# Residual of the second half in a place of its own, and copies for two sets of weight sums, both issued ahead of the first half's MLP products

## The chip, the cores and the metric

The kernel runs on one core of one Trainium2 chip. The core has a matrix engine (TensorE, PE, with its weight loads as PEld), a vector engine (DVE), a scalar engine (ACT), GpSimd (POOL) and SyncE (SP), which here does nothing but issue DMAs. Sixteen DMA engines move the data. DMAs are issued from two places: SP (the queue called SPq, hardware_dynamic) and POOL (POOLq, software_dynamic). Each engine works through its own instructions in order and waits on semaphores for the others. The metric is the device time of one launch in microseconds (us); lower is better.

## What is computed

A trunk of two layers on 1024 tokens of width 1024, in float32. Layer 0 mixes tokens with a gated linear recurrence, layer 1 with a causal Conformer convolution; each mixer is followed by a squared-ReLU MLP of inner width 4096, with a residual and a layer norm after each.

```python
for i in range(DEPTH):
    if i % N_MIXERS == 0:
        mix = hgrn2_mixer(x, ...)
    else:
        mix = conformer_conv_mixer(x, ...)
    x = layer_norm(DEEPNORM_ALPHA * x + mix, ln_mix_g[i], ln_mix_b[i])
    ff = jnp.square(jax.nn.relu(x @ ffn_w1[i])) @ ffn_w2[i]
    x = layer_norm(DEEPNORM_ALPHA * x + ff, ln_ffn_g[i], ln_ffn_b[i])

def conformer_conv_mixer(h, w_pw1, b_pw1, w_dw, b_dw, ln_g, ln_b, w_pw2, b_pw2):
    a, gate = jnp.split(h @ w_pw1 + b_pw1, 2, axis=-1)
    u = a * jax.nn.sigmoid(gate)
    u = depthwise_causal_conv(u, w_dw) + b_dw          # 31 taps
    u = jax.nn.silu(layer_norm(u, ln_g, ln_b))
    return u @ w_pw2 + b_pw2
```

The change lies in layer 1. The residual that it speaks of is `DEEPNORM_ALPHA * x` in front of the first of the two norms.

## The kernel before

**Numbers.** Every float32 factor of a product is split into a high part and a remainder, and each product is three matmuls: high by high, high by low, low by high (`product`, line 329). One such matmul, with a tile of 128x128 and 512 columns, is what the profile calls `ps<-xa,wa` and the like. 24 of them, eight tiles of the inner dimension by three, make one 128x512 result.

**Fewer products.** The large products are cut into 2x2 blocks and done with seven block products in place of eight; the seven "forms" are numbered in `ORDER` (line 45). Forms 6, 5, 7 and 3 of a weight are sums of its four blocks. For the second MLP weight w2 these sums are made in DRAM, one set for each of the eight column groups of each layer: `block_sums` (line 393) copies blocks into a DRAM tile of four places (`sum_w` in the profile) with two plain DMAs of 1 MB, and adds to it with three accumulating DMAs, which POOL issues. The list `to_sum` (line 408) has sixteen sets. Fourteen are made in layer 0, the last two, groups 6 and 7 of layer 1, later. Where the argument `after` is given, a marker comes first: a DMA of two elements from `after` into the tile, which holds the copies back until `after` has been written. They then go through SP's queue.

**Layer 1** works on two halves of 512 tokens, `half` 0 and 1. The string `SEQ` (line 40) gives the order of its steps, and the loop at line 1680 runs them:

- P0j and P1j: the pointwise input product of channel block j. It leaves behind the convolution of that block as background work: 19 taps on DVE, 12 taps that ACT multiplies and POOL adds. The result is turned by PE into `ct[half]`, the tile `y` of 16 KB a partition.
- N, F, S: `normalise` (line 1554), the layer norm of the convolution; `finish` (line 1579), which turns it back and applies SiLU into `sT[half]`; `second` (line 1600), the output product with w_pw2, the residual and the norm. The weights of all these steps come through `wa` (a `Slots` object, line 60; six places of 8 KB).
- UA0 to UA4: the first half's MLP up-products `up_half(1, i, 0, ...)` for column groups 0 to 4, four blocks of w1 each. They fill PE while the second half's convolution runs in the background. Thirteen of the w1 blocks lie already split in DRAM (`ready`): two DMAs of 512 KB each, with no work on ACT or DVE. Block k of UA is loaded as `wa` has a free place, six blocks behind the one that used it.
- E, UB and L: the first two forms of the remaining groups for the first half, the second half's up-products for groups 0 to 4, and groups 5 to 7 for both halves. The down-products with w2 follow.

**Places.** SBUF is laid out by hand in KB of a partition (`view`, line 274). `ct[0]` lies at 32 to 48, `ct[1]` at 48 to 64. After its last turn in `finish`, `ct[half]` is loaded anew with the residual from `kept[half]` in DRAM, four DMAs of 512 KB on SP (line 1596); `second` scales it by ALPHA and adds the bias on DVE (line 1605), adds each product and normalises in place. Later tiles take the same places over: `xf6` at 32, `s7` at 48, `first` at 56, and the slots of the last MLP.

**Order.** After line 1019 the order of the instructions on each engine is not the program's: a scheduler places them by its own simulated time. Only the order on each engine is fixed so; what an engine waits for is decided by semaphores. Consecutive DMAs of SP take eight semaphores in turn, so that a DMA also waits for the landing of the eighth before it. In layer 1 the order of the steps on PE is P00 to P17 (with N0, F0, S0 in between), then UA0 to UA4, N1, F1 and S1 (with E5 to E7 in between), then UB0.

Of the kernel before, what the change touches and what calls it, by code (L numbers as in the profile page):

```python
# [8 lines left out]
F32 = mybir.dt.float32  # L9
# [3 lines left out]
ALU = mybir.AluOpType  # L13
# [249 lines left out]
def body(ctx, tc, d, out):  # L263
# [126 lines left out]

    sums = {}

    def block_sums(name, layer, c, after=None, gap=0):

        t = sums[name, layer, c] = dram.tile([4, P, 1024], F32, name=f"sum_{name}{layer}{c}")
        v, w = t.rearrange("a p n -> p a n"), d[name][layer, c].rearrange("a p n -> p a n")
        queue = nc.sync if after is not None else nc.gpsimd
        if after is not None:
            nc.sync.dma_start(out=t[0:4:2, 0, 0:1], in_=after)
        queue.dma_start(out=v[:, 0:2], in_=w[:, 0:4:2])  # L400
        later(gap // 2, lambda: queue.dma_start(out=v[:, 2:4], in_=w[:, 0:2]))
        parts = [lambda: nc.gpsimd.dma_start(out=v[:, 0:2], in_=w[:, 2:4], accum_op=ALU.add)]
        for i in (2, 3):
            parts.append(lambda i=i: nc.gpsimd.dma_start(out=v[:, i], in_=v[:, i - 1], accum_op=ALU.add, max_dma_last_dim=4096))
        for i, part in enumerate(parts):
            later((i + 1) * gap, part)
# [817 lines left out]
    class LateUp(Up):  # L1224


        def __init__(self, xs):
            self.layer, self.xf = 1, xs
            self.zs, self.ws = bank((1, 5, 2, 6)), bank((3, 7, 0, 4))
            self.c = ring((132, 134, 136, 138, 128, 130), wide_t, "c")  # L1230
            self.hr = ring((16, 24, 0, 8), (2, 2, HT), "hr")
            self.t = ring(run(112, 4, 2), (2, 256), "ht")
            self.p = ring((56,), (2, HT), "first")
            self.of = {}

        def bring(self, c):
# [317 lines left out]
    def normalise(half):  # L1554

        for job in conv[KB * half : KB * half + KB]:
            bg.flush(job)
        while late:
            late.pop(0)()
        mv = stat.tile([P, NTB, 5], F32, tag="mv4", name="mv", bufs=2)  # L1560
        for t in range(NTB):
            vector.bn_aggr(mv[:, t, 0:2], cs[half][:, t])
        vector.tensor_scalar(out=mv[:, :, 2:3], in0=mv[:, :, 1:2], scalar1=LN_EPS, scalar2=None, op0=ALU.add)
        nc.gpsimd.tensor_tensor(out=mv[:, :, 3:4], in0=mv[:, :, 2:3], in1=nhalf[:, :NTB].rearrange("p (a b) -> p a b", b=1), op=ALU.pow)
        vector.scalar_tensor_tensor(out=mv[:, :, 4:5], in0=mv[:, :, 0:1], scalar=-1.0, in1=mv[:, :, 3:4], op0=ALU.mult, op1=ALU.mult)
        normed[0] = 1
        if half == 1:
            for of in to_sum:
                block_sums(*of, mv[:2, 0, 4:5])
        gate[1] = [mv[:, 0, 4:5]] * 2  # L1570
        for n in range(2):
            for t in range(NTB):
                cv = ct[half][:, t, n * HT : (n + 1) * HT]
                if n == 0 and t % 2:
                    vector.tensor_scalar(out=cv, in0=cv, scalar1=mv[:, t, 3:4], scalar2=mv[:, t, 4:5], op0=ALU.mult, op1=ALU.add)
                else:
                    nc.scalar.activation(cv, cv, AF.Identity, bias=mv[:, t, 4:5], scale=mv[:, t, 3:4])

    def finish(half):

        st = sT[half]

        def one(j):
            pt = rings["aux"]()
            for t in range(NTB):
                tensor.transpose(pt[:, t * P : (t + 1) * P], ct[half][:, t, j * P : (j + 1) * P], ident)
            z = big("z")
            sg = big("r")
            gj, bj = par[:, CLG + j : CLG + j + 1], par[:, CLB + j : CLB + j + 1]
            nc.scalar.activation(sg, pt, AF.Sigmoid, bias=bj, scale=gj)  # L1590
            nc.scalar.activation(z, pt, AF.Identity, bias=bj, scale=gj)
            vector.tensor_tensor(out=z, in0=z, in1=sg, op=ALU.mult)
            split(st[:, 0, j, :], st[:, 1, j, :], z)
            if j == KB - 1:
                for t in range(NTB):
                    nc.sync.dma_start(out=ct[half][:, t, :], in_=kept[half][t])

        bg.chores += [lambda j=j: (one(j), one(j + 1)) for j in range(0, KB, 2)]

    def second(half):  # L1600

        y = ct[half]
        bp2 = vec(184, "b_pw2", 0)
        for t in range(NTB):
            vector.scalar_tensor_tensor(out=y[:, t, :], in0=y[:, t, :], scalar=ALPHA, in1=bp2, op0=ALU.mult, op1=ALU.add)
        if half == 1:
            x3T[1] = half_x(144, "xc")
        xt = x3T[half]
        g, b = gain(184, "ln_mix", 1)

        def back(t):
            turn(y[:, t, :], xt, t, 0, KB)

        for n, t in ((n, t) for n in range(2) for t in range(NTB)):
            if t == 0:
                w = wa.take(4)
                wa.ahead(2)
            ps = acc()
            product(ps, wide(sT[half], t, w))
            yv = y[:, t, n * HT : (n + 1) * HT]  # L1620
            vector.tensor_tensor(out=yv, in0=yv, in1=ps, op=ALU.add)
            if n == 1:
                norm(y[:, t, :], g, b)
                keep(half, t, y[:, t, :])
                bg.chores.append(lambda t=t: back(t))

    def late_forms():

        a, x = x3T
        x6, s7 = view(32, (2, 4, HT), F32R, "xf6"), view(48, (4, HT), F32, "s7")  # L1630
        scratch = ring((140, 216), (2, HT), "s")
        xs = {6: x6, 5: a[:, :, :4], 4: a[:, :, 4:], 7: x[:, :, :4], 3: x[:, :, 4:]}

        def part(t, i, k):
            return t[:, i, k : k + 2].bitcast(F32)

        def less(o, p, q):
            vector.tensor_tensor(out=o, in0=p, in1=q, op=ALU.subtract)

        def minus_both(o, p, t, k):  # L1640
            vector.scalar_tensor_tensor(out=o, in0=p, scalar=-1.0, in1=part(t, 0, k), op0=ALU.mult, op1=ALU.subtract)
            less(o, o, part(t, 1, k))

        def cut_form(i, k, s):
            cut(xs[i][:, 0, k : k + 2], xs[i][:, 1, k : k + 2], s)

        def both(o, s, t, k1, u, k2):
            less(o, part(t, 0, k1), part(u, 0, k2))
            less(s, part(t, 1, k1), part(u, 1, k2))
            vector.tensor_tensor(out=o, in0=o, in1=s, op=ALU.add)  # L1650

        jobs = []
        for k in (0, 2):
            s, r = scratch(), scratch()

            def fifth(k=k, s=s, r=r):
                both(s, r, a, k, x, k)
                cut_form(5, k, s)

            def sixth(k=k, s=s, r=r):  # L1660
                minus_both(r, s, x, 4 + k)
                cut_form(6, k, r)

            def seventh(k=k, s=s, r=r):
                both(s7[:, k : k + 2], s, x, 4 + k, x, k)

            def fourth(k=k, s=s, r=r):
                minus_both(s, r, a, 4 + k)
                cut_form(4, k, s)

            jobs += [fifth, sixth, seventh, fourth]

        def end():
            for k in (0, 2):
                cut_form(7, k, s7[:, k : k + 2])

        bg.chores.extend(jobs)
        return xs, end

    for op, i in steps:  # L1680
# [15 lines left out]
        elif op == "S":  # L1696
            second(i)
        elif op == "UA":
            up_half(1, i, 0, wa, stA, x3T[0])
        elif op == "E":  # L1700
            soon(i, wa, stA, {1: x3T[0][:, :, :4], 2: x3T[0][:, :, 4:]})
        elif op == "UB":
# [4 lines left out]
                xs, last_form = late_forms()  # L1707
            if i == NEAR - 1:
                bg.done()
                lf = LateForms(nc, vector, slots((104, 200, 208, 96, 192), "fw"), raws((176, 180, 216, 140)), raws((60,), "sum"))  # L1710
                lf.todo = [[(blocks("w1q", 1, c),)] for c in range(NEAR, NFC)]
                lf.ahead(1)
            up_half(1, i, 1, wa, stB, x3T[1])
# [5 lines left out]
        else:  # L1719
# [3 lines left out]
            for k in LATER:  # L1723
                (f,) = lf.take(1)
                lf.ahead(3)
                up.form(i, k, f)
                if i == NFC - 1 and k == 6:
                    fw = Slots(nc, vector, slots([32, 104, 200, 208, 144, 152, 160], "dw"), raws([56, 176, 180, 60, 140, 136], "dr"))
                    fh = Slots(nc, vector, slots([40, 48, 0, 8, 64, 72, 80], "dh"))
                    plan_down(1, fw, fh)  # L1730
                if i == NFC - 1 and k in (6, 5):
                    fw.ahead(1 if k == 6 else 2)
                    fh.ahead(1 if k == 6 else 2)
# [91 lines left out]
```

## Time and profile before

| | us |
|---|---|
| median of 3 runs | 2090.7 |
| lowest and highest | 2089.12 and 2091.88 |
| profiled execution, its time | 2092.44 |
| its span, first to last instruction | 2090.7 |

The mean granted clock of TensorE in the profiled execution is 0.994 of full speed. Times in the views are microseconds from the start of the span. A row of a timeline has the start, the duration, the engine, the line of the kernel, the operation, out<-in by the program's names, the shape and the count of merged instructions, and in brackets how long the engine had been idle and what ended that. SPq rows are DMA issues: their duration is SP's, not that of the transfer. Line L198 is that of a helper through which PE, DVE and POOL are recorded, so there one goes by the names of the tiles: `y` is the residual and later the sum, `wa` the weights, `xa` and `xc` the split inputs of the MLP, `ha` the MLP's inner activations, `cb` a convolution result, `sum_w` the sums of w2, `kept` the residual in DRAM. A DMA view lists packets and bytes of each queue, and the issues with their size and the median time to landing.

### The profile page before, as it was taken

To read this page: it belongs to the slowest core of one execution; us is meant where nothing else is said; L and a number is where in the kernel's file an instruction comes from. 1 tells how busy PE (TensorE), PEld (TensorE's weight loads), DVE (VectorE), ACT (ScalarE), POOL (GpSimd) and SP (SyncE) were. 2 spreads that over 40 slices of the span, in tenths; PEclk is the share of its full clock that TensorE was granted. 3 is DMA by queue.
4 is the path that set the end of the run, shared out by engine and by line. 5 is a ranking of instruction groups with operands and counts; after the bars stand their busy time and mean duration, and the time that the engine had idled before them with its cause. 6 is when DMAs were issued, how large, how long until landed. Compare 5 with 4: busy or idle time off the path is not lost.

```text
span 2090.7 us, 29408 instructions
## 1 busy us (share of the span) xinstructions
PE 2050.0 (98%) x11136; PEld 1692.0 (81%) x11136; DVE 1474.6 (71%) x1929; ACT 1079.4 (52%) x1678; POOL 400.0 (19%) x393
## 2 busy tenths in 40 slices
PE   8999999999999999999999999999979999999998
PEld 7878887888888888888888888888867888888886
DVE  8598887877776666565667997899349657554456
ACT  5456565632565556444454767377514456433433
POOL 0112222111000000000002996497010000000002
PEclk9999999999999999999999999999999999999999
DMA  4778999842789767989988654763877988955542
GB/s 184 221 194 243 256 243 271 247 164 81 206 298 308 273 223 257 407 314 333 342 312 317 222 195 168 283 248 125 271 252 253 336 289 282 374 195 191 193 160 101
DMA packets 178830, 513.85 MB, mean 246 GB/s; under 512 B 17152, under 2 KB 47488, under 8 KB 177664
## 3 DMA queue, kind: packets, MB, share of 16 engines
q1 hardware_dynamic: 163200, 453.25, 61.2%
q0 software_dynamic: 15488, 58.72, 12.3%
q8 instruction: 87, 1.43, 0.3%
q14 instruction: 55, 0.45, 0.1%
HBM read 378.22 MB, written 200.80 MB: 277 GB/s over the span
## 4 chain that ended last, share of the span: by engine, by line
PE 56%; POOL 3%; DMA 3%; DVE 2%; ACT 1%; issue 1%; DVEq 0%; POOLq 0%; SPq 0%
PE ps L198 56%; POOL cb L198 3%; DMA wa<-ready 1%; DMA dh<-hf 1%; DMA y<-kept 1%; DVE y L198 1%; ACT prod L1516 0%; DVE wa L198 0%; ACT hr L1179 0%; ACT c L1178 0%; DMA raw<-in_w_dram 0%; DVE bs L198 0%; ACT dh L72 0%; DVE ht L198 0%; ACT wa L72 0%
## 5 line engine op out<-in xcount | busy, mean ns | idle before, releaser
L198 PE MATMUL ps<-dw,dh 128*128 128x512 f32 x2688 | 611.6, 389 | 0.9 <-ACT dh L72 0.9
L198 PEld LDWEIGHTS ps<-dw,dh 128*128 128x128 f32 x2688 | 504.1, 188 | 105.8 <-ACT dh L72 1.3
L198 PE MATMUL ps<-x1f,fw 128*128 128x512 f32 x1344 | 308.5, 390 | 1.1 <-DVE c L198 0.8
L198 PEld LDWEIGHTS ps<-x1f,fw 128*128 128x128 f32 x1344 | 251.3, 188 | 54.0 <-issue 1.2
L198 PE MATMUL ps<-xf,fs 128*128 128x512 f32 x1008 | 250.8, 400 | 1.3 <-DVE t L198 0.9
L198 POOL TENSOR_TENSOR cb<-cb,prod 128x512 f32<-128x512 f32 x176 | 234.3, 1340 | 17.6 <-ACT prod L1516 7.1
L198 PE MATMUL ps<-xa,wa 128*128 128x512 f32 x1008 | 234.8, 391 | 0.0
L198 DVE TENSOR_TENSOR dh<-dh 128x1024 fp32r<-128x1024 f32 x112 | 136.6, 1222 | 121.9 <-ACT dh L72 121.6
L198 PEld LDWEIGHTS ps<-xa,wa 128*128 128x128 f32 x1008 | 187.6, 188 | 38.2
L198 PEld LDWEIGHTS ps<-xf,fs 128*128 128x128 f32 x1008 | 185.0, 189 | 40.6 <-DVE t L198 2.1
L198 DVE SCALAR_TENSOR_TENSOR ps<-u,par,ps 128x512 f32<-128x512 f32 x288 | 198.6, 749 | 9.8 <-ACT ps L1528 8.4
L198 DVE TENSOR_TENSOR dw<-dr,dw 128x1024 fp32r<-128x1024 f32 x112 | 136.5, 1222 | 86.3 <-ACT dw L72 86.0
L72 ACT CAST dh<-dh 128x1024 fp32r<-128x1024 f32 x112 | 117.1, 1050 | 148.5 <-DMA dh<-hf 146.3
L72 ACT CAST dw<-dr 128x1024 fp32r<-128x1024 f32 x112 | 117.4, 1052 | 135.2 <-PE ps L198 124.8
L1516 ACT ACTIVATE prod<-u,par 128x512 f32<-128x512 f32 x176 | 125.4, 722 | 54.0 <-POOL cb L198 53.4
L499 POOL TENSOR_TENSOR mv<-mv,nhalf 128x1 f32<-128x1 f32 x32 | 46.3, 1448 | 456.9 <-DVE mv L198 456.9
L198 PE MATMUL ps<-xc,wa 128*128 128x512 f32 x480 | 110.6, 393 | 0.0
L198 PEld LDWEIGHTS ps<-xc,wa 128*128 128x128 f32 x480 | 91.1, 190 | 19.3 <-ACT xc L1026 0.2
L1377 POOL COPY next<-ss 128x1 f32<-128x1 f32 x37 | 21.2, 574 | 406.1 <-DVE spare L198 256.8
L198 PE MATMUL ps<-w,oT 128*128 128x512 f32 x384 | 89.3, 391 | 0.8 <-ACT oT L913 0.8
L198 PE MATMUL ps<-xb,wa 128*128 128x512 f32 x384 | 89.3, 391 | 0.0
L198 PE MATMUL ps<-vw,xf 128*128 128x512 f32 x336 | 79.8, 398 | 6.4 <-ACT vw L416 5.1
(227 smaller groups left out, 2809.6 us busy)
## 6 DMA issues: line engine op xcount, KB each, us to landing
wa<-ready SPq DMA_DIRECT2D x122, 512.0 KB, 4.6
dh<-hf SPq DMA_DIRECT2D x112, 512.0 KB, 5.6
sum_w<-in_w_dram POOLq DMA_DIRECT2D x40, 1024.0 KB, 10.4
ready<-spare SPq DMA_DIRECT2D x74, 512.0 KB, 5.0
dr<-sum_w SPq DMA_DIRECT2D x64, 512.0 KB, 4.2
raw<-in_w1q_dram SPq DMA_DIRECT2D x54, 512.0 KB, 4.9
dr<-in_w_dram SPq DMA_DIRECT2D x48, 512.0 KB, 5.2
hf<-ht SPq DMA_DIRECT2D x88, 256.0 KB, 5.0
```

The lines of the kernel that those rows point to most:

```text
L72: self.nc.scalar.copy(out=slot[:, 0, c], in_=raw[:, c])
L198: return op(*args, **kw)
L499: nc.gpsimd.tensor_tensor(out=dst, in0=src, in1=nhalf[:, :n], op=ALU.pow)
L1377: nc.gpsimd.tensor_copy(out=raw[:, :1], in_=now)
L1516: nc.scalar.activation(tp, u[:, k : k + HT], AF.Copy, scale=tap(j, k))
```

## The change

Two things move to the start of step UA0, in front of its products.

First, the residual of half 1. `residual_of(1, ...)` loads it there, into a view at 32 to 48 KB, the place of the first half's `ct[0]`. `second(1)` works in that place, in `rest[1]`, in place of `ct[1]`. The residual of half 0 is loaded at the end of `finish(0)` as before. The tiles that took over 32 to 48 and 48 to 64 exchange places.

Second, the two copies of each of the last two sets of sums. At UA0 they are made for rows 1 to 127, behind a marker from the last element of `x3T[0]` (`xa`). Row 0 is copied at N1, behind a marker from the norm's `mv`, and there the accumulating DMAs are issued too. In all there are four copies of 127 rows, four of one row (two runs of 4 KB each), and four markers in place of two.

```diff
--- before.py
+++ after.py
@@ -390,11 +390,24 @@
 
     sums = {}
 
-    def block_sums(name, layer, c, after=None, gap=0):
+    def block_sums(name, layer, c, after=None, gap=0, adds=None):
 
         t = sums[name, layer, c] = dram.tile([4, P, 1024], F32, name=f"sum_{name}{layer}{c}")
         v, w = t.rearrange("a p n -> p a n"), d[name][layer, c].rearrange("a p n -> p a n")
         queue = nc.sync if after is not None else nc.gpsimd
+        if adds is not None:
+
+            def copies(rows, after):
+                nc.sync.dma_start(out=t[0:4:2, rows.start, 0:1], in_=after)
+                queue.dma_start(out=v[rows, 0:2], in_=w[rows, 0:4:2])
+                queue.dma_start(out=v[rows, 2:4], in_=w[rows, 0:2])
+
+            copies(slice(1, P), after)
+            adds.append(lambda after: copies(slice(0, 1), after))
+            adds.append(lambda after: nc.gpsimd.dma_start(out=v[:, 0:2], in_=w[:, 2:4], accum_op=ALU.add))
+            for i in (2, 3):
+                adds.append(lambda after, i=i: nc.gpsimd.dma_start(out=v[:, i], in_=v[:, i - 1], accum_op=ALU.add, max_dma_last_dim=4096))
+            return
         if after is not None:
             nc.sync.dma_start(out=t[0:4:2, 0, 0:1], in_=after)
         queue.dma_start(out=v[:, 0:2], in_=w[:, 0:4:2])
@@ -1230,7 +1243,7 @@
             self.c = ring((132, 134, 136, 138, 128, 130), wide_t, "c")
             self.hr = ring((16, 24, 0, 8), (2, 2, HT), "hr")
             self.t = ring(run(112, 4, 2), (2, 256), "ht")
-            self.p = ring((56,), (2, HT), "first")
+            self.p = ring((40,), (2, HT), "first")
             self.of = {}
 
         def bring(self, c):
@@ -1565,8 +1578,8 @@
         vector.scalar_tensor_tensor(out=mv[:, :, 4:5], in0=mv[:, :, 0:1], scalar=-1.0, in1=mv[:, :, 3:4], op0=ALU.mult, op1=ALU.mult)
         normed[0] = 1
         if half == 1:
-            for of in to_sum:
-                block_sums(*of, mv[:2, 0, 4:5])
+            for add in adds:
+                add(mv[:2, 0, 4:5])
         gate[1] = [mv[:, 0, 4:5]] * 2
         for n in range(2):
             for t in range(NTB):
@@ -1575,6 +1588,13 @@
                     vector.tensor_scalar(out=cv, in0=cv, scalar1=mv[:, t, 3:4], scalar2=mv[:, t, 4:5], op0=ALU.mult, op1=ALU.add)
                 else:
                     nc.scalar.activation(cv, cv, AF.Identity, bias=mv[:, t, 4:5], scale=mv[:, t, 3:4])
+
+    def residual_of(half, y):
+        for t in range(NTB):
+            nc.sync.dma_start(out=y[:, t, :], in_=kept[half][t])
+        rest[half] = y
+
+    rest, adds = [None, None], []
 
     def finish(half):
 
@@ -1591,15 +1611,14 @@
             nc.scalar.activation(z, pt, AF.Identity, bias=bj, scale=gj)
             vector.tensor_tensor(out=z, in0=z, in1=sg, op=ALU.mult)
             split(st[:, 0, j, :], st[:, 1, j, :], z)
-            if j == KB - 1:
-                for t in range(NTB):
-                    nc.sync.dma_start(out=ct[half][:, t, :], in_=kept[half][t])
+            if j == KB - 1 and half == 0:
+                residual_of(half, ct[0])
 
         bg.chores += [lambda j=j: (one(j), one(j + 1)) for j in range(0, KB, 2)]
 
     def second(half):
 
-        y = ct[half]
+        y = rest[half]
         bp2 = vec(184, "b_pw2", 0)
         for t in range(NTB):
             vector.scalar_tensor_tensor(out=y[:, t, :], in0=y[:, t, :], scalar=ALPHA, in1=bp2, op0=ALU.mult, op1=ALU.add)
@@ -1627,7 +1646,7 @@
     def late_forms():
 
         a, x = x3T
-        x6, s7 = view(32, (2, 4, HT), F32R, "xf6"), view(48, (4, HT), F32, "s7")
+        s7, x6 = view(32, (4, HT), F32, "s7"), view(48, (2, 4, HT), F32R, "xf6")
         scratch = ring((140, 216), (2, HT), "s")
         xs = {6: x6, 5: a[:, :, :4], 4: a[:, :, 4:], 7: x[:, :, :4], 3: x[:, :, 4:]}
 
@@ -1696,6 +1715,10 @@
         elif op == "S":
             second(i)
         elif op == "UA":
+            if i == 0:
+                residual_of(1, view(32, (NTB, D), F32, "y"))
+                for of in to_sum:
+                    block_sums(*of, x3T[0][:2, 1, KB - 1, HT - 1 :].bitcast(F32), adds=adds)
             up_half(1, i, 0, wa, stA, x3T[0])
         elif op == "E":
             soon(i, wa, stA, {1: x3T[0][:, :, :4], 2: x3T[0][:, :, 4:]})
@@ -1707,7 +1730,7 @@
                 xs, last_form = late_forms()
             if i == NEAR - 1:
                 bg.done()
-                lf = LateForms(nc, vector, slots((104, 200, 208, 96, 192), "fw"), raws((176, 180, 216, 140)), raws((60,), "sum"))
+                lf = LateForms(nc, vector, slots((104, 200, 208, 96, 192), "fw"), raws((176, 180, 216, 140)), raws((44,), "sum"))
                 lf.todo = [[(blocks("w1q", 1, c),)] for c in range(NEAR, NFC)]
                 lf.ahead(1)
             up_half(1, i, 1, wa, stB, x3T[1])
@@ -1725,8 +1748,8 @@
                 lf.ahead(3)
                 up.form(i, k, f)
                 if i == NFC - 1 and k == 6:
-                    fw = Slots(nc, vector, slots([32, 104, 200, 208, 144, 152, 160], "dw"), raws([56, 176, 180, 60, 140, 136], "dr"))
-                    fh = Slots(nc, vector, slots([40, 48, 0, 8, 64, 72, 80], "dh"))
+                    fw = Slots(nc, vector, slots([48, 104, 200, 208, 144, 152, 160], "dw"), raws([40, 176, 180, 44, 140, 136], "dr"))
+                    fh = Slots(nc, vector, slots([56, 32, 0, 8, 64, 72, 80], "dh"))
                     plan_down(1, fw, fh)
                 if i == NFC - 1 and k in (6, 5):
                     fw.ahead(1 if k == 6 else 2)
```

## Prediction

> **What bounds the kernel now.** I read first the page's busy times, then the list of what TensorE (PE) waited for, then 20 us windows around the change, and last the timeline and the DMA issues of the stage in which PE stands.
>
> ```profile
> span 2090.7 us, 29408 instructions
> ...
> PE 2050.0 (98%) x11136; PEld 1692.0 (81%) x11136; DVE 1474.6 (71%) x1929; ACT 1079.4 (52%) x1678; POOL 400.0 (19%) x393
> ```
>
> PE is busy for 98% of the span. An edit that leaves its products alone can gain at most the 40 us of idle time, but whatever makes PE wait is paid in full. PE's waits, as total, count and longest:
>
> ```profile
> PE ps L198 <- DVE y L198: 11.0, 2, 10.5
> ...
> PE ps L198 <- DVE xc L198: 3.7, 3, 2.3
> ```
>
> The wait of 10.5 us lies in S1, the second half's output product. Windows (length, then busy time of PE, PEld, DVE, ACT, POOL, granted clock, DMA share, GB/s):
>
> ```profile
> 1520.00:1540.00 20.00, 10.18 (x45) 8.07 (x44) 2.33 (x3) 2.10 (x2) 1.76 (x3) 0.87 1.05 303
> 1540.00:1560.00 20.00, 18.04 (x68) 14.12 (x69) 10.81 (x15) 0.00 (x0) 0.70 (x1) 0.88 0.70 235
> 1600.00:1620.00 20.00, 20.00 (x90) 16.57 (x89) 18.71 (x17) 9.69 (x14) 0.00 (x0) 1.00 0.69 239
> ```
>
> PE stands for 9.8 us while the DMA engines are full, and then works at a lower granted clock: 18.04/68 = 265 ns a product against 20.00/90 = 222, so 68 products cost 2.9 us more. The timeline names the chain, and the DMA issues from 1440 to 1600 us (size, median us to landing) its cause:
>
> ```profile
> 1537.66 1.23 DVE L198 SCALAR_TENSOR_TENSOR y<-y,b_pw 128x1024 f32<-128x1024 f32 x1 [18.43 <-DMA y<-kept]
> ...
> 1540.68 4.96 PE L198 MATMUL ps<-wa,xb 128*128 128x512 f32 x12 [10.50 <-DVE y L198]
> ...
> 1549.95 10.27 PE L198 MATMUL ps<-wa,xb 128*128 128x512 f32 x44 [0.84 <-DMA wa<-ready]
> ```
>
> ```profile
> wa<-ready SPq DMA_DIRECT2D x16, 512.0 KB, 17.9
> ...
> sum_w<-in_w_dram SPq DMA_DIRECT2D x4, 1024.0 KB, 13.1
> ...
> y<-kept SPq DMA_DIRECT2D x4, 512.0 KB, 26.0
> ```
>
> The residual (y<-kept) takes 26 us because four 1 MB copies (sum_w) stand before it in the same queue.
>
> **What the change takes away.** Residual and copies leave this stage, so the waits on y and on the weights behind them, 11.0 + 0.84 = 11.8 us, and the lower clock after them (2.9) should go, 14.7 in all. The order of the changed program also spreads the transposes at the end of S1, for which PE waits 3.7 us; I count 1.3 of it. Gain 16 us. Lower end: 3, if the weights are late instead; upper: 20, with all of the 3.7 and some clock.
>
> **What it adds: where the transfers now stand.** In the changed program SP's queue reads, behind UA0's fourth weight block: two markers, the four loads of the residual, blocks 5 and 6 (UA1's first two), the four copies, then blocks 7, 8 and so on. In the trace of before, the last write of xa on DVE, SP's issues of blocks 6 and 7 (two loads each), and UA's first products on PE:
>
> ```profile
> 1362.35 0.68 DVE L198 TENSOR_TENSOR xa<-ps,xa 128x512 fp32r<-128x512 f32 x1
> ```
>
> ```profile
> 1369.30 0.80 SPq L81 DMA_DIRECT2D wa<-ready  x2
> ...
> 1375.23 0.79 SPq L81 DMA_DIRECT2D wa<-ready  x2
> ```
>
> ```profile
> 1369.69 15.49 PE L198 MATMUL ps<-xa,wa 128*128 128x512 f32 x67
> 1385.02 0.60 PE L198 MATMUL ps<-ident,cb 128*128 128x128 f32 x4
> 1385.38 0.71 PE L198 MATMUL ps<-xa,wa 128*128 128x512 f32 x2
> 1385.92 0.60 PE L198 MATMUL ps<-ident,cb 128*128 128x128 f32 x4
> 1386.28 17.30 PE L198 MATMUL ps<-xa,wa 128*128 128x512 f32 x75
> ```
>
> A block feeds 24 products. 67 + 2 + 75 = 144 products use up six blocks, so PE needs block 7 at about 1403.4 us. The markers wait for xa, complete at 1363.0; the copies are issued behind block 6, at about 1370; block 7 waits for its slot until 1375.2 and lands behind the copies. Nothing that PE does before 1403.4 is delayed.
>
> **The price of the copies.** Each moves 127 rows x 2 x 4 KB = 1.04 MB; row 0 is left for later. No such transfer is in the trace of before, where all large ones have 128 rows. The nearest rows, for packets:
>
> ```profile
> DMA packets 288, 1.05 MB, mean 194 GB/s; under 512 B 32, under 2 KB 32, under 8 KB 288
> ...
> wa<-ready SPq DMA_DIRECT2D x2, 512.0 KB, 4.2
> ```
>
> ```profile
> DMA packets 170, 0.61 MB, mean 166 GB/s; under 512 B 20, under 2 KB 20, under 8 KB 170
> ...
> raw<-in_w1q_dram SPq DMA_DIRECT2D x2, 512.0 KB, 3.6
> sum_w<-in_w_dram SPq DMA_DIRECT2D x1, 1024.0 KB
> sum_w<-fw SPq DMA_DIRECT2D x1, 0.0 KB
> ```
>
> Both are DMA views, of 1375.2 to 1380.6 us and of 536.8 to 540.5 us. In the first, two loads of 128 rows leave 2 x 128 packets of 4 KB and 32 small ones: sixteen small packets each, one completion from every engine. In the second one load completes (16), and a marker (sum_w<-fw, two rows of 4 bytes) adds only 4: two of data, two completions. So the marker ran on two engines, not on sixteen: the number of engines follows from the rows, in equal shares. 127 is prime; equal shares leave one engine. I take that end, and keep the even spread as a rival.
>
> The Trainium skill, "DMA: Bandwidth & Descriptors", section "Why a DMA increments its semaphore by 16 and not by 1", has the rule: on SP's and ACT's path a transfer runs on the largest number of engines up to 16 that divides the slowest dimension of both sides, and 127 partitions is one of its examples of a single engine. The trace agrees for the two rows above; it holds no 127. By this rule the sum is the one below, without it the first rival's.
>
> What one engine carries, from a window full of loads and from a DMA view (1496 to 1500 us) filled mainly by such copies:
>
> ```profile
> 1355.00:1360.00 5.00, 5.00 (x28) 4.24 (x27) 5.00 (x10) 3.99 (x7) 4.77 (x5) 1.00 1.03 418
> ```
>
> ```profile
> DMA packets 380, 1.45 MB, mean 364 GB/s; under 512 B 25, under 2 KB 25, under 8 KB 380
> ```
>
> 418/16/1.03 = 25.4 GB/s, so 41.0 us a copy; 364/16 = 22.8 GB/s gives 45.7. I take the first, since one engine alone meets no crowd: four copies 164 us (slow end 183; spread over sixteen engines 4.2 MB at 418 GB/s, 10 us).
>
> **When block 7 lands.** The markers go at 1363.0, then the residual's four loads at 0.4 us each. From about 1364.7 us the engines have the residual (2.1 MB) and blocks 5 and 6 (2.1 MB) ahead of the copies: 10 us at 418 GB/s, start 1374.7. The copies end at 1538.5. Every 128-row load has a sixteenth on that same engine, behind them: block 7's 64 KB take 2.6 us, landing some 2 more (a load alone needs 4.2 us for 1.3 us of transfer). PE gets it at 1543, after 140 us of standing. Behind it the next blocks need 2.5 us each against 5.4 of products, so they keep up. The first products cost 2.9 us of low clock again (ends 0 and 6).
>
> **What costs nothing.** Convolution, sigmoids and squares run on DVE, ACT and POOL, but ACT meets the activation of the block that PE has not made and stops; the stage is shifted whole. The four scalings of y (1.23 us each) now stand among the convolution's DVE work, hidden by the standstill; without it DVE has little room:
>
> ```profile
> 1380.00:1400.00 20.00, 20.00 (x93) 16.55 (x92) 18.97 (x30) 16.70 (x28) 18.98 (x15) 1.00 0.60 210
> ```
>
> There they cost PE up to 4 x 1.23 = 4.9 us, taken as 2. The row-0 copies at N1 are two rows of 4 KB each, like markers; the accumulating DMAs behind them start no later than before relative to N1, and their sums are read in the last MLP. The exchanged places in SBUF move no work.
>
> **Sum.** 140 + 2.9 - 16 = +127 us: span 2090.7 + 127 = 2218, or 2219 for the profiled execution (2092.4, 1.7 above its span). The median of the runs shown equals the span, so I predict 2218. Own range: fast end with copies starting at 1370 (-5), gain 20 (-4) and no clock loss (-3), 2206; slow end with 183 us of copies (+19), gain 11, the waits without the clock (+5), 2242.
>
> **Rivals.**
> 1. The copies spread over sixteen engines (other side). For: the 13.1 us of their 128-row form; against: the marker's 4 packets. They would be through by about 1386, block 7 by 1390, before 1403.4; only the gain is left: 2090.7 - 16 + 2 = 2077. It decides from the point where four copies take under about 25 us together. The same time results if later loads overtake the copies on that engine; against: wa<-ready took 17.9 us behind the copies of before, 4.2 alone.
> 2. The change doesn't do what it says for S1: its weights (17.9 us to landing) become the wait in place of y. For: the wait of 0.84 on them already there; against: 6 MB less in that queue. Gain 3: 2231.
> 3. One engine, but at the slow rate of the crowded copies: 2090.7 + 159 + 2.9 - 16 = 2237.
>
> **How the numbers follow.** Forecast 0.66, rival 1 with its overtaking form 0.14, rival 2 0.09, rival 3 0.11. From 2198 to 2248 the range holds forecast, rivals 2 and 3 and 5 us beyond their ends, about 0.8 in all, and leaves rival 1 out. Faster than 2086.5 (0.2%, about what a measurement of this kernel can tell from no change): 0.14; within 0.2%: 0.01, the chance that a small stall cancels the gain; slower: 0.85.
>
> **What would show it.** Right: one PE wait of about 140 us on wa<-ready in UA1, a DMA share near 0.06 and 26 GB/s beside it, the four copies landing 41 us after one another, no wait on y in S1. Wrong at the engine count: copies landing within 15 us and no such wait; wrong at the gain: S1 still waits over 5 us.

## The result and the profile after

The changed kernel takes 2209.0 us, median of 4 runs (2206.36 to 2210.84), against 2089.9 us of the kernel before in the same comparison (2088.32 to 2091.88): the ratio is 1.0568 [1.0550, 1.0587], slower. The profiled execution took 2208.82 us, 116.3 us more span than before, at a mean granted clock of 0.968. From the page of the changed kernel, the span and the busy times:

```profile
span 2207.0 us, 29411 instructions
...
PE 2047.1 (93%) x11136; PEld 1690.1 (77%) x11136; DVE 1477.4 (67%) x1929; ACT 1079.7 (49%) x1678; POOL 398.0 (18%) x393
```

PE does the same work (2047.1 us busy, 2050.0 before) with 119 us more of idle time. Its waits (total, times, longest) say where:

```profile
PE ps L198 <- DMA wa<-ready: 133.9, 2, 132.2
...
PE ps L198 <- ACT xc L1039: 0.3, 1, 0.3
```

The waits on y and on DVE's xc (11.0 and 3.7 us before) are gone. One wait for weights of 132.2 us has come; the timeline of PE puts it in UA1, where block 7 is needed:

```profile
1391.98 12.54 PE L198 MATMUL ps<-xa,wa 128*128 128x512 f32 x54
1536.74 15.17 PE L198 MATMUL ps<-xa,wa 128*128 128x512 f32 x55 [132.22 <-DMA wa<-ready]
```

The windows of the changed kernel show what moves meanwhile (length, PE, PEld, DVE, ACT, POOL, granted clock, DMA share, GB/s):

```profile
1400.00:1420.00 20.00, 4.52 (x20) 3.39 (x19) 18.87 (x29) 11.80 (x19) 17.65 (x14) 0.71 0.06 26
1420.00:1440.00 20.00, 0.00 (x0) 0.00 (x0) 0.00 (x0) 0.00 (x0) 0.00 (x0) 0.50 0.06 26
...
1520.00:1540.00 20.00, 3.24 (x7) 2.17 (x8) 0.00 (x0) 0.00 (x0) 0.00 (x0) 0.50 0.70 253
1540.00:1560.00 20.00, 20.00 (x91) 16.42 (x90) 11.56 (x16) 14.15 (x23) 11.64 (x9) 0.96 0.78 292
...
1660.00:1680.00 20.00, 18.28 (x82) 14.78 (x80) 11.78 (x17) 2.11 (x2) 2.37 (x2) 1.00 0.70 219
```

A share of 0.06 is one engine of sixteen (1/16 = 0.0625), and it moves 26 GB/s. The DMA view of 1400 to 1500 us says the same a second way:

```profile
DMA packets 647, 2.64 MB, mean 26 GB/s; under 512 B 3, under 2 KB 3, under 8 KB 647
```

In 100 us there are 644 packets of 4 KB, one every 155 ns, and only 3 small ones: read as one completion for each copy that ends, where a 128-row load leaves sixteen. Last, the timeline of SP (start, time in the issue itself):

```profile
1371.09 0.71 SPq L402 DMA_DIRECT2D sum_w<-in_w_dram  x1
1371.85 31.23 SPq L403 DMA_DIRECT2D sum_w<-in_w_dram  x1
1403.12 39.56 SPq L402 DMA_DIRECT2D sum_w<-in_w_dram  x1
1442.72 39.56 SPq L403 DMA_DIRECT2D sum_w<-in_w_dram  x1
1482.39 40.70 SPq L81 DMA_DIRECT2D wa<-ready  x2
```

Each issue behind the first copy holds SP, the later ones for the length of a whole copy, 39.56 us. The eight semaphores that SP's DMAs take in turn are not the reason: the eighth DMA before each copy is a load of the residual, before block 7's a load of block 5, and the engines were through with both by 1380 (their share from 1380 to 1400 us is 0.07). A queue that is full fits, but no view shows the queue itself. Block 7 is the last row: its two loads were being issued from 1482.4 to 1523.1, over 100 us late. The Trainium skill, "DMA: Bandwidth & Descriptors", section "Why a DMA increments its semaphore by 16 and not by 1", gives one engine to 127 partitions; the share, the rate and the single completions agree.

### The profile page after: what moved, and what is told of

Read it like the earlier page. It is cut to its first block, busy times and chain, and to the rows that moved or that the text cites. A ratio compares the mean times of both kernels' runs of the same rounds, so it can differ in the third digit from the quotient of the medians.

```text
span 2207.0 us, 29411 instructions
## 1 busy us (share of the span) xinstructions
PE 2047.1 (93%) x11136; PEld 1690.1 (77%) x11136; DVE 1477.4 (67%) x1929; ACT 1079.7 (49%) x1678; POOL 398.0 (18%) x393
## 4 chain that ended last, share of the span: by engine, by line
PE 60%; another core or an unknown queue 6%; DMA 1%; issue 0%; ACT 0%; DVE 0%; POOL 0%; DVEq 0%; SPq 0%; POOLq 0%
PE ps L198 60%; DMA wa<-ready 0%; DVE y L198 0%; ACT hr L1192 0%; ACT c L1191 0%; DMA next<-in_wpw_dram 0%; DVE fw L198 0%; DVE c L198 0%; ACT spare L1383 0%; POOL next L1390 0%; ACT fw L72 0%; DVE bs L198 0%; DVE ht L198 0%; DVEq L1844 0%
## 5 line engine op out<-in xcount | busy, mean ns | idle before, releaser
L198 PE MATMUL ps<-xa,wa 128*128 128x512 f32 x1008 | 237.7, 394 | 132.2 <-DMA wa<-ready 132.2
L1295 ACT ACTIVATE r<-ps 128x512 f32<-128x512 f32 x40 | 23.6, 590 | 155.9 <-PE ps L198 155.9
```

The costliest lines, as they stand in the source:

```text
L198: return op(*args, **kw)
L1295: nc.scalar.activation(r, ps, AF.Relu)
```

## The experiments

The theory: the whole loss is the price of a row count that lets only one DMA engine work; with a row count that divides by sixteen the change gains. The rivals: the place costs (bulk copies in front of weights that PE needs soon); the residual, not the copies, costs; SP alone costs, not the DMA engine's order.

### The same copies over 112 rows

Against the changed kernel; the order on PE and SP stays the same.

```diff
-            copies(slice(1, P), after)
-            adds.append(lambda after: copies(slice(0, 1), after))
+            copies(slice(16, P), after)
+            adds.append(lambda after: copies(slice(0, 16), after))
```

> The changed kernel with 112 rows copied at UA0 and 16 at N1, in place of 127 and 1; the order of all instructions is the same. Theory (a transfer runs on the largest number of engines up to 16 that divides its rows, so 127 rows have one engine, and all later loads of SP's queue stand behind it): 112 rows have sixteen engines, the copies take about 10 us together, the standstill of 132 us on wa<-ready is gone, and what is left is the gain of S1, about 18 us (132.2 + 2.3 us of low clock - 116.3 us of longer span): about 2072 us. Rival (the copies' bytes and place are the cause: 4 MB of copies and 2 MB of residual in front of the weights): the bytes are nearly the same, so the standstill stays: about 2190 to 2207 us.

Measured: 2081.4 us (2078.61 to 2084.74), ratio 0.9948 [0.9932, 0.9964]. One row number in the code turns 119 us of loss into 11 us of gain. SP's timeline, the window of 1380 to 1400 us, and PE's waits from 1340 to 1760 us:

```profile
1372.46 0.58 SPq L402 DMA_DIRECT2D sum_w<-in_w_dram  x1
...
1377.55 1.18 SPq L81 DMA_DIRECT2D wa<-ready  x2
```

```profile
1380.00:1400.00 20.00, 20.00 (x94) 16.57 (x93) 16.90 (x22) 13.89 (x23) 18.52 (x14) 1.00 0.99 354
```

```profile
PE ps L198 <- DVE cb L198: 3.6, 2, 3.1
PE ps L198 <- DMA wa<-ready: 3.4, 2, 1.8
```

SP is held for 0.6 us a copy, block 7 is issued at 1377.6, all sixteen engines work (share 0.99, copies and block loads together), and no standstill is left. But the time stands 9 us above the 2072 expected. One part is a wait of 3.6 us on cb, a convolution result, of which the kernel before had 0.3 and the changed one nothing; the experiment on the scalings below takes it up. The weights of S1 are 3.4 us late, 1.7 more than in the changed kernel. The other 4 us are not divided further.

### Each part alone

The residual's early place without the early copies (the copies as before, at N1), and the early copies over 112 rows with the residual loaded at its old place and time.

Against the changed kernel, residual alone:

```diff
         if half == 1:
-            for add in adds:
-                add(mv[:2, 0, 4:5])
+            for of in to_sum:
+                block_sums(*of, mv[:2, 0, 4:5])
...
                 residual_of(1, view(32, (NTB, D), F32, "y"))
-                for of in to_sum:
-                    block_sums(*of, x3T[0][:2, 1, KB - 1, HT - 1 :].bitcast(F32), adds=adds)
```

Copies alone (the exchanged places are put back too):

```diff
-            copies(slice(1, P), after)
-            adds.append(lambda after: copies(slice(0, 1), after))
+            copies(slice(16, P), after)
+            adds.append(lambda after: copies(slice(0, 16), after))
...
-            if j == KB - 1 and half == 0:
-                residual_of(half, ct[0])
+            if j == KB - 1:
+                for t in range(NTB):
+                    nc.sync.dma_start(out=ct[half][:, t, :], in_=kept[half][t])
...
-        y = rest[half]
+        y = ct[half]
...
-                residual_of(1, view(32, (NTB, D), F32, "y"))
                 for of in to_sum:
```

> The residual comes early to the place of its own; the copies stay at N1 with 128 rows, as before. Theory: no standstill in UA; S1 no longer waits for y, but its weights still stand behind the four copies, so only part of the 18 us is gained: a PE wait on wa<-ready in S1 of some 5 us, about 2083 us. Rival (the residual in front of the weights is itself late or harmful): a wait in UA1, 2095 us or more.

> The copies come early (112 rows, then 16 at N1); the residual comes back to the old place in S1 as before. Theory: no standstill; the residual's loads no longer stand behind copies and land in about 8 us instead of 26, so the wait on y shrinks from 10.5 us to 2 or less: about 2077 us. Rival (bytes and place): a standstill on wa<-ready in UA1 of over 50 us.

Measured: the residual alone 2086.3 us (2081.83 to 2090.57), ratio 0.9971 [0.9961, 0.9982]; the copies alone 2081.2 us (2079.52 to 2084.97), ratio 0.9952 [0.9935, 0.9969]. Both parts gain, 6.2 and 11.3 us against the 2092.5 of the kernel before beside them. PE's waits in the same stretch, of the residual alone and then of the copies alone:

```profile
PE ps L198 <- DMA wa<-ready: 4.1, 1, 4.1
PE ps L198 <- DVE cb L198: 3.6, 2, 3.1
```

```profile
PE ps L198 <- DVE y L198: 4.0, 2, 2.4
PE ps L198 <- DVE xc L198: 1.5, 3, 1.0
```

Both fell short of what was expected, 2083 and 2077 us. With the residual alone the wait of 4.1 us on the weights is about the 5 expected, and the wait on cb was not expected. With the copies alone the residual's loads landed after 15.1 us (median), not 8, and the longest wait on y is 2.4 us. The two together (11.1 us) gain no more than the copies alone. The waits show that the gains overlap: moving the copies already shortens the wait on y from 11.0 to 4.0 us; moving the residual too removes the rest and the 1.5 us on xc, but brings the wait on cb (3.6 against 0.4) and 3.1 us more on the weights (3.4 against 0.3).

### Rows against engines: 122 and 124

Against the 112-row kernel, the split at another row.

```diff
-            copies(slice(16, P), after)
-            adds.append(lambda after: copies(slice(0, 16), after))
+            copies(slice(6, P), after)
+            adds.append(lambda after: copies(slice(0, 6), after))
```

```diff
-            copies(slice(16, P), after)
-            adds.append(lambda after: copies(slice(0, 16), after))
+            copies(slice(4, P), after)
+            adds.append(lambda after: copies(slice(0, 4), after))
```

> The changed kernel with 122 rows at UA0 and 6 at N1, same order of instructions. Theory (largest divisor up to 16 of 122 is 2): two engines, 122 packets of 155 ns on each, 18.9 us a copy, four from 1377 to 1453 us, so PE stands from 1404 to about 1456: 51 us, and 2090 + 51 + 2 - 18 = 2125 us. If an odd row count only costs a tail (sixteen engines, the last with fewer rows): no standstill, 2072. If bytes and place are the cause: 2200 or more.

> The changed kernel with the early copies over 124 rows and the late ones over 4. Theory (equal shares of the rows over the largest number of engines up to 16 that divides them): four engines, 62 packets of 4 KB each at the 154.6 ns measured in the changed kernel, 9.6 us a copy, 38 us in all, from about 1377 to 1415 us; block 7 lands near 1418 against 1403.4 needed, so PE stands about 14 us there, and the time is the 2081 us of the 112-row kernel + 14 + 2 = 2097 us. DMA share near 0.25 and about 105 GB/s during the copies. Rival (the rows are dealt out one by one over sixteen engines unless their number is prime or twice a prime): 2081 us and no such wait.

Measured, in one run each: 2126.7 us with 122 rows and 2091.6 with 124. The window of 1380 to 1400 us and PE's wait on the weights, for 122 rows and then for 124:

```profile
1380.00:1400.00 20.00, 20.00 (x94) 16.56 (x93) 16.92 (x25) 15.44 (x26) 18.46 (x15) 1.00 0.13 53
```

```profile
PE ps L198 <- DMA wa<-ready: 53.8, 3, 51.3
```

```profile
1380.00:1400.00 20.00, 20.00 (x94) 16.57 (x93) 16.91 (x24) 14.73 (x25) 18.52 (x14) 1.00 0.26 106
```

```profile
PE ps L198 <- DMA wa<-ready: 16.3, 3, 13.8
```

A share of 0.13 is two engines, 0.26 four: the largest numbers up to sixteen that divide 122 = 2 x 61 and 124 = 4 x 31. The bandwidth goes 26, 53, 106 GB/s with one, two and four engines, and the longest wait 132.2, 51.3, 13.8 us. Neither "spread unless prime" nor a fixed sixteen fits. By the Trainium skill, "DMA: Bandwidth & Descriptors", section "Why a DMA increments its semaphore by 16 and not by 1", the engines would be 1, 2, 4 and 16 for 127, 122, 124 and 112 rows, and the DMA shares of 0.06, 0.13, 0.26 and 0.99 agree, the last with block loads beside the copies. With 122 rows the time is the 2125 us expected. With 124 rows it is 5 us under the expected one, which was built on the 2081 us of the 112-row kernel. There is no wait on cb here, 3.6 us less; that DVE catches up while PE stands is the likely reason, not one that was tried.

### The row count at the old place

The kernel before, with its copies of the two sets cut into 127 rows and one row where they are.

```diff
-        if after is not None:
-            nc.sync.dma_start(out=t[0:4:2, 0, 0:1], in_=after)
-        queue.dma_start(out=v[:, 0:2], in_=w[:, 0:4:2])
-        later(gap // 2, lambda: queue.dma_start(out=v[:, 2:4], in_=w[:, 0:2]))
+        for rows in (slice(1, P), slice(0, 1)) if (name, layer) == ("w2", 1) and c >= 6 else (slice(0, P),):
+            if after is not None:
+                nc.sync.dma_start(out=t[0:4:2, rows.start, 0:1], in_=after)
+            queue.dma_start(out=v[rows, 0:2], in_=w[rows, 0:4:2])
+            later(gap // 2, lambda rows=rows: queue.dma_start(out=v[rows, 2:4], in_=w[rows, 0:2]))
```

> The kernel before, residual and copies at their old place, but the copies of the two sets cut into 127 rows and 1 row there. Theory (the price hangs on the row count, not on the place): SP is held about 40 us in each of the later copies, and the loads behind them in its queue, weights and residual, land some 140 us late; PE stands 120 to 145 us near 1510 to 1680 us; about 2220 us (2200 to 2240). Rival (the place at UA0 is what costs, in front of blocks that PE needs soon): near 2090 us.

Measured: 2237.0 us in one run. SP's timeline and PE's waits:

```profile
1492.38 28.90 SPq L402 DMA_DIRECT2D sum_w<-in_w_dram  x1
1521.38 39.50 SPq L401 DMA_DIRECT2D sum_w<-in_w_dram  x1
```

```profile
PE ps L198 <- DMA wa<-ready: 138.2, 2, 137.8
PE ps L198 <- DVE y L198: 18.4, 2, 18.1
```

The same copies at another place hold SP for the same 39.5 us and cost PE as much. The rival of the place falls.

### One copy of 127 rows

Of the four early copies, the first alone has 127 rows, the others 112. Against the 112-row kernel:

```diff
-            def copies(rows, after):
+            def copies(rows, after, one):
...
-                queue.dma_start(out=v[rows, 0:2], in_=w[rows, 0:4:2])
+                queue.dma_start(out=v[one, 0:2], in_=w[one, 0:4:2])
...
-            copies(slice(16, P), after)
-            adds.append(lambda after: copies(slice(0, 16), after))
+            first = (slice(1, P), slice(0, 1)) if c == NFC - 2 else (slice(16, P), slice(0, 16))
+            copies(slice(16, P), after, first[0])
+            adds.append(lambda after: copies(slice(0, 16), after, first[1]))
```

> The changed kernel with only the first of the early copies over 127 rows, the three others and the late ones over 112 and 16. Theory (a load takes its turn on each DMA engine behind what was issued before it): the copy holds one engine from about 1377 to 1416 us; the three others and block 7 have their sixteenths on that engine behind it, 3 x 14 + 16 packets of 154.6 ns, 9 us; block 7 lands near 1426, needed at 1403.4: PE stands about 22 us, near 2081 + 22 + 2 = 2105 us, even where SP itself is not held for a copy's length. Rival (it is only SP, held in the issue, that makes the loads late, and a load issued in time overtakes): block 7 lands within 10 us of its issue, no standstill, 2081 us.

Measured: 2096.6 us in one run. SP's timeline, and PE's:

```profile
1370.65 31.25 SPq L403 DMA_DIRECT2D sum_w<-in_w_dram  x1
...
1406.95 3.69 SPq L81 DMA_DIRECT2D wa<-ready  x2
```

```profile
1424.22 14.56 PE L198 MATMUL ps<-xa,wa 128*128 128x512 f32 x55 [20.91 <-DMA wa<-ready]
```

The wait of 20.9 us is the 22 expected; the time is 8 us under the 2105 expected, of which the missing wait on cb is 3.6. The wait alone doesn't tell the two theories apart: one such copy is enough to hold SP, so block 7 was not issued in time. From the start of its issue to PE's restart (1406.95 to 1424.22) went 17 us, more than the 10 us that the rival allowed, while the other copies, 3 x 112 rows x 8 KB = 2.75 MB, moved just before it.

The trace of the changed kernel tells more. There the issue of block 7's first load ended at 1521.9 us. Two DMA views, of 1523.9 to 1524.5 us and of 1534.9 to 1536.4 us:

```profile
DMA packets 55, 0.16 MB, mean 273 GB/s; under 512 B 15, under 2 KB 15, under 8 KB 55
```

```profile
DMA packets 14, 0.05 MB, mean 33 GB/s; under 512 B 2, under 2 KB 2, under 8 KB 14
```

The fifteen small packets in the first are read as the completions of that load on fifteen engines. In the second one engine works almost alone and completes two things, the last copy and then the load's sixteenth share; PE starts again at 1536.74. So a load that is already issued waits its turn on the slow engine, here some 12 us, and SP's hold is not all of the price.

### The scalings of y bound to N1

Against the 112-row kernel: ALPHA is computed from the norm's `mv` by one more small instruction, so that the four scalings can't run before N1.

```diff
-        normed[0] = 1
+        normed[:] = 1, mv
...
         bp2 = vec(184, "b_pw2", 0)
+        al = normed[1][:, 0, 2:3]
+        vector.tensor_scalar(out=al, in0=normed[1][:, 0, 4:5], scalar1=0.0, scalar2=ALPHA, op0=ALU.mult, op1=ALU.add)
         for t in range(NTB):
-            vector.scalar_tensor_tensor(out=y[:, t, :], in0=y[:, t, :], scalar=ALPHA, in1=bp2, op0=ALU.mult, op1=ALU.add)
+            vector.scalar_tensor_tensor(out=y[:, t, :], in0=y[:, t, :], scalar=al, in1=bp2, op0=ALU.mult, op1=ALU.add)
```

> The changed kernel with 112 and 16 rows, and the four scalings of y bound to the norm's result at N1 (ALPHA comes as a factor computed from mv), so that they no longer stand among the convolution's work on DVE. Theory (the scalings cost PE the wait on cb of 3.6 us that the 112-row kernel shows): no wait on cb, 2081.4 - 3.6 = about 2078 us, below the 112-row kernel. Rival (the wait on cb comes from the other work on DVE or from the transfers beside it, not from the scalings): 2081 to 2082 us with the wait on cb still there.

> The 112-row kernel once more, beside the gated one on the same chip. Both theories: 2081 us (ratio 0.9948), wait on cb near 3.6 us.

> The gated kernel once more beside the ungated one. Theory (the scalings in the convolution cost PE 3 to 5 us): its time is 3 to 5 us under that of the 112-row kernel of this call, with ratios whose intervals lie apart. Rival (the gain in the first run was that of a chip): both within 1.5 us.

Measured: 2076.4 us (2071.62 to 2079.46), ratio 0.9921 [0.9907, 0.9935]. In the second comparison, beside each other: 112 rows 2081.5 us (2080.20 to 2083.93), ratio 0.9947 [0.9933, 0.9961]; with the gate 2078.5 us (2074.33 to 2079.47), ratio 0.9927 [0.9915, 0.9940]. The scalings in the 112-row kernel (its view of the tile y; ns as least, median and most), and in the first gated run the scalings on the timeline of DVE and PE's waits:

```profile
L198 DVE SCALAR_TENSOR_TENSOR y<-y,b_pw x4: 1559/1650/2252, 1376.4 to 1384.3; 128x1024 f32<-128x1024 f32 x4
```

```profile
1485.36 4.87 DVE L198 SCALAR_TENSOR_TENSOR y<-y,mv,b_pw 128x1024 f32<-128x1024 f32 x4
```

```profile
PE ps L198 <- DMA wa<-ready: 3.0, 2, 1.8
PE ps L198 <- DVE cb L198: 0.4, 1, 0.4
```

Ungated, the scalings stand at 1376 to 1386 us among the convolution's work and take 1.56 to 2.25 us each, 7.1 in all; gated they run at 1485 us, after the convolution, and the wait on cb falls from 3.6 to 0.4 us. The wait on cb follows the scalings in every changed version here without a standstill: 3.6 to 3.7 us where they stand early (112 rows twice, residual alone), 0.4 where they stand late (copies alone, gated twice). In the second comparison the time falls by 3.0 us, the least of the 3 to 5 expected, and the intervals, which were expected apart, overlap a little. The gate also shifts some of the scheduler's other choices on PE, SP and DVE, so not all of the 3 us need be the scalings. This version is the fastest here, 14 to 17 us under the kernel before.

## Why the prediction was right

Predicted were 2218 us, measured 2209.0, inside the range of 2198 to 2248. In the span, 2207.0 us against the sum's 2217.6, the 10.6 us between them are 7.8 of the standstill, 0.5 of the restart and 2.3 of the gain. All three err to the same side; only within the standstill do two small errors hide each other.

**Engine count.** Right, and the step on which all depended. It was read from packet counts of rows that weren't 127; the row counts of 122, 124 and 112 now fit the rule too, and the old place shows that the early place is not needed for the loss.

**Length of a copy.** Mis-sized a little: 41.0 us by 418 GB/s over 16 engines and the share 1.03; measured 39.56, by SP's issues. The busy window gave an engine's rate beside fifteen others; alone it was 3.5% quicker. Four copies: 5.8 us less.

**The standstill.** 140 predicted, 132.2 measured. Of the 7.8 us, 5.8 are the copies; 1.1 is PE's stop at 1404.5 (1391.98 + 12.54) in place of 1403.4. The last 0.9 is two errors against each other: by the small packets of the trace the last copy was done at 1535.0, so that the four began near 1377 in place of 1374.7, and PE started 1.7 us behind the last copy's end, not 4.6.

**Restart.** 2.9 us predicted; 55 products in 15.17 us are 276 ns each, against 12.54/54 = 232 just ahead of the stop: 2.4 us.

**The gain.** 16 predicted. Worked back from the span: 132.2 + 2.4 - 116.3 = 18.3 us. By its terms: the y wait 11.0; the weights in S1 got 0.9 worse, not 0.8 better (133.9 - 132.2 = 1.7 against 0.84); the clock term is met, since S1 now works at 18.28/82 = 223 ns at full clock, 2.9; the wait on xc fell by 3.4 (3.7 to 0.3), of which 1.3 was counted. Sum 16.4. The last 1.9 us do not lie in waits: all waits but the standstill fell by 13.0 us, 0.5 less than the three terms on waits make (11.0 - 0.9 + 3.4). They lie in PE's busy time, which fell from 2050.0 to 2047.1 although the restart added 2.4. That is 5.3 us less without the restart, 2.4 more than the clock term; where in the stage stays open.

**What costs nothing.** The freeze is in the changed kernel's timelines of ACT, POOL and DVE, just as argued:

```profile
1414.43 0.72 ACT L1529 ACTIVATE prod<-u,par 128x512 f32<-128x512 f32 x1 [0.62 <-POOL cb L198]
1544.91 0.60 ACT L1295 ACTIVATE r<-ps 128x512 f32<-128x512 f32 x1 [129.75 <-PE ps L198]
...
1546.26 4.04 POOL L198 TENSOR_TENSOR cb<-cb,prod 128x512 f32<-128x512 f32 x3 [127.83 <-ACT prod L1529]
...
1547.95 0.76 DVE L198 SCALAR_TENSOR_TENSOR ps<-u,par,ps 128x512 f32<-128x512 f32 x1 [129.05 <-ACT ps L1541]
```

ACT waits for the product that PE has not made, and DVE and POOL wait for ACT. The scalings of y: hidden, as said, while PE stands (no wait on cb in the changed kernel); without the standstill they cost about 3 us by the last experiment, between the 2 taken and the bound of 4.9. The bound itself was too low: it counted 1.23 us for each, and there the four took 7.1 us.

**Rivals.** Even spread (2077): the wrong engine count, but its time is near what the change yields once the rows allow it, 2081 us, or 2076 to 2078 with the scalings gated. Later loads overtaking: not seen; most of the time they weren't issued, as the next point says, and block 7's, once issued, still waited for the slow engine. S1's weights in place of y: they are late by 1.7 us only. The crowded rate of 45.7 us a copy: excluded by 39.56.

**What the prediction did not see.** It put block 7's loads in the engine's queue behind the copies, issued at about 1375. They stood in SP instead, which was held in the issues of the copies, and were in the queue only from 1521.9 on. This step of the path was wrong. That it cost the number nothing is luck: with four equal copies on one engine, held in SP or queued, the loads come behind the last of them.

## What to carry to other kernels

Before cutting a transfer by rows, look at the divisors of what is left: 127 + 1 rows run on one DMA engine and 112 + 16 on sixteen, and here that was 2209 against 2081 us. A slow transfer isn't only late itself: everything behind it in its queue is late, so look for long issues in the timeline of the issuing engine. Work moved early should be followed to the engine that must do it there; four scalings on a nearly full DVE cost up to about 3 us until they were tied to a later result.

## What the runs showed of the hardware

A DMA issue on SP is not always short: behind a transfer on one engine it took 39.56 us, with two engines up to 18.44 (122 rows), with four up to 9.87 (124 rows), and 0.58 with sixteen; with few engines, at the longest, about as long as one copy lasts. The first such copy is issued in 0.71 us and the second is held at once (31.23 us): if a full queue is the reason, its room is less than two copies of 127 rows. What is held need not be large: the first load of block 7, with a sixteenth of its 512 KB for that engine, was held for 39.47 us.

The timelines of SP with 122 rows and with 124:

```profile
1380.97 18.44 SPq L402 DMA_DIRECT2D sum_w<-in_w_dram  x1
```

```profile
1373.64 9.87 SPq L402 DMA_DIRECT2D sum_w<-in_w_dram  x1
```

The granted clock stood at 0.50 all through the standstill and at 0.96 in the window of 1540 to 1560 us, so that 132 us of standing cost no more at the restart than the 9.8 us before. The scalings of y took 1.56 to 2.25 us each beside the convolution and a full set of loads, and 1.23 in S1 before; what slows them there was not tried.
